# MLP and SwiGLU stages with two classical tile pairs instead of four, and seven-product units behind them

## The chip, the cores and the metric

The kernel runs on one core of a Trainium2 chip. Its time is device microseconds of one execution, from the first to the last instruction with what lies around them; of several runs the median is taken. TensorE (PE in the rows) multiplies, VectorE (DVE) and ScalarE (ACT) work on tiles of 128 partitions, GpSimd (POOL) issues accumulating DMAs and SyncE (SP) plain ones. Each engine works through its own list of instructions in order and waits on semaphores for the others.

## What is computed

Two networks, one after the other, on a sequence of 512 tokens with 1024 channels, in float32. The change touches four places of it, two squared-relu MLPs and two SwiGLU layers:

```python
def squared_relu_mlp(h, w_up, w_down):
    u = jax.nn.relu(h @ w_up)              # 1024 -> 4096, in both layers of the first block
    return (u * u) @ w_down
...
def swiglu_ffn(x, g, w_gate, w_up, w_down):
    h = rms_norm_2(x, g)
    return (jax.nn.silu(h @ w_gate) * (h @ w_up)) @ w_down   # 1024 -> 2816, before and after the mixer
```

Each is added to the residual stream, and before the second network there is a norm with its own gain. Around them stand a stick-breaking attention, a retention layer and a mixer, which the change leaves as they are.

## The kernel before

Activations lie transposed: a tile is 128 channels by 512 tokens, and the stream is eight tiles `hh[0]` to `hh[7]`. Every float32 operand is split into a rounded high part (ScalarE, `whi` or `.hi`) and the remainder (VectorE, `wlo` or `.lo`), and a product is three matmuls, high by low, low by high and high by high (`mm3`, lines 125 to 127).

A **classical tile** (`g_unit`) is 8 k-tiles by 3 matmuls with 512 columns; a pair of tiles is 48 of these. A **unit** (`w_unit`) makes a pair of tiles by the seven products of a Strassen-Winograd scheme on 2 by 2 blocks: seven products, each 4 k-tiles by 3 matmuls with 256 columns, 84 in all, accumulated in four PSUM banks (`ps_z`) with copies between banks on ScalarE (`before(x)`, L337 to L345). It needs two kinds of operands made of sums. The weight side is summed for each panel: two sums by accumulating DMAs from GpSimd (L210, L211), two by VectorE (L263), each then split (L272, L232). The activation side is made once for a stage by `w_operands`, in four groups of two k-tiles: ScalarE lifts two tiles by their gain (L496), VectorE makes four sums (L310 to L313), ScalarE rounds two (L316, L317), VectorE makes two remainders (L319, L320). `w_operands` is a generator with four steps for each group. The weave calls it at every `WT`-th step of the main program; a step is one k-tile of a classical tile (three matmuls) or half a product of a unit (six matmuls).

In a stage the first tile pairs are classical, since the operands for units are not there yet: all four pairs of an MLP's first group of eight tiles, and the first four gate-and-up pairs (`GC`) of a SwiGLU. After them what is left of `w_operands` is drained (`for _ in ops: pass`), and all later pairs are units. The finish of a tile (`up_done`: in an MLP relu L549, square L550, split L172 and L173; in a SwiGLU L1004 to L1006 and the split) is put off by `later` for a few steps. The norm's factor comes while the first tiles run: a sum over partitions on TensorE (L444), a reciprocal root in some twenty tiny VectorE instructions (L425 to L431), a spread over the partitions on TensorE (L437), a copy on ScalarE (L473).

In the first SwiGLU stage, `residual` multiplies the eight tiles of the stream by a second norm's factor (L1789) when the operands are drained (`after()`).

Where an instruction stands in its engine's list is decided by a scheduling framework from dependencies and the order of the program; the lists below come from the built programs. Weight panels are loaded two ahead into three buffers (`RAWS = 3`), and their preparation runs up to `WAHEAD = 5` products ahead.

Of the kernel before, what the change touches and what calls it, by code (L numbers as in the profile page):

```python
# [12 lines left out]
ALU = mybir.AluOpType  # L13
# [41 lines left out]

WAHEAD = 5

WT = 3

GC = 4  # L60


CHUNKS = {
# [23 lines left out]
class Builder:  # L87
# [451 lines left out]
    def mlp(self, layer, hh, X, box, nxt):  # L539

        nc = self.nc
        st = {}
        self.norm_soon(st, box)
        U = {}


        def up_done(m, ps):
            z = self.h()
            nc.scalar.activation(z, ps, AF.Relu)  # L549
            nc.scalar.activation(z, z, AF.Square)  # L550
            U[m] = self.split(z)

        def pair_done(m):
            lo, hi = slice(0, 256), slice(256, 512)
            y, z = self.h(), self.h()

            def d11(c11):
                nc.scalar.activation(y[:, lo], c11, AF.Relu)

            def d12(p, q):  # L560
                nc.vector.tensor_tensor(y[:, hi], p, q, ALU.add)
                nc.vector.scalar_tensor_tensor(y, y, 0.0, y, ALU.max, ALU.mult)

            def d22(p, q):
                nc.vector.tensor_tensor(z[:, hi], p, q, ALU.add)

            def d21(c21):
                nc.scalar.activation(z[:, lo], c21, AF.Relu, scale=-1.0)
                nc.scalar.activation(z[:, hi], z[:, hi], AF.Relu, scale=-1.0)
                nc.scalar.activation(z, z, AF.Square)  # L570
                U[m] = self.split(y)
                U[m + 1] = self.split(z)
            return d11, d12, d22, d21

        def down_done(grp, m, ps):
            if "R2" not in st:
                st["R2"] = self.h()
                nc.vector.tensor_tensor(st["R2"], st["R"], st["R"], ALU.mult)
            t = self.h()
            nc.vector.tensor_tensor(t, ps, st["R2"], ALU.mult)  # L580
            nc.vector.tensor_tensor(hh[m], hh[m], t, ALU.add)
            if grp == 3:
                nxt(m)

        T = []
        ops = self.w_operands(X, T, lambda k: self.lifted(hh[k], self.g(f"mlp{layer}", k)))
        banks = self.w_banks(X[0].hi)

        def main():
            for grp in range(4):  # L590
                for m in range(0, 8, 2):
                    if grp == 0:
                        for x in range(2):
                            yield from self.g_unit(f"up{layer}", X[::2] + X[1::2])
                            self.later(up_done, m + x, self.last)
                    else:
                        yield from self.w_unit(f"up{layer}", T, banks, pair_done(m))
                if grp == 0:
                    for _ in ops:
                        pass  # L600
                self.flush()
                W = [U[m] for m in range(8)]
                for m in range(8):
                    yield from self.g_unit(f"dn{layer}", W)
                    self.later(down_done, grp, m, self.last)

        self.weave(main(), [[ops, WT]])
        self.flush()

# [385 lines left out]
    def ffn(self, which, hh, X, st, nxt, lift, after=lambda: None):  # L995
# [49 lines left out]
        def main():  # L1045
            for gi, grp in enumerate((range(0, 8), range(8, 16), range(16, 22))):
                for i in grp:
                    if i < GC:
                        yield from self.g_unit(f"gu{which}", X[::2] + X[1::2])
                        pg = self.last  # L1050
                        yield from self.g_unit(f"gu{which}", X[::2] + X[1::2])
                        self.later(up_done, i, pg, self.last)
                        if i == GC - 1:
                            for _ in ops:
# [20 lines left out]

        self.weave(main(), [[ops, WT]])
        self.flush()
# [589 lines left out]
    def build(self):  # L1667
        nc = self.nc
        P = self.panels
# [6 lines left out]

        def mlp(l):
            for g in range(4):
                P(f"up{l}", range(g * 4, g * 4 + 4), g > 0)
                P(f"dn{l}", range(g * 4, g * 4 + 4))  # L1680

        def ffn(w):
            for g in range(2):
                for i in range(g * 8, g * 8 + 8):
                    P(f"gu{w}", [i], i >= GC)
                P(f"fd{w}", range(g * 4, g * 4 + 4))
            P(f"gu{w}", range(16, 22), True)
            P(f"fe{w}", range(4))

        mlp(0)  # L1690
        for h in range(4):
            P("retqk", [2 * h, 2 * h + 1])
            P("retv", [2 * h, 2 * h + 1])
            P("retg", [2 * h, 2 * h + 1])
            if h >= 2:
                P("reto", range((h - 2) * 4, (h - 2) * 4 + 4))
        mlp(1)
        ffn(1)
        P("small", [0])
# [42 lines left out]
        def ready(gain, X, hh=None):  # L1742

            def f(m, h):
                self.sumsq(box, m, h)
                X.append(self.gain_in(h, self.g(gain, m)))
            return f if hh is None else lambda m: f(m, hh[m])
# [3 lines left out]
        hh = self.sb(ready("mlp0", X))  # L1751
# [33 lines left out]

        def residual():
            R1 = self.bcast(st["r1"])
            for kt in range(KT):
                nc.vector.scalar_tensor_tensor(hh[kt], hh[kt], self.g("fin", kt), R1, ALU.mult, ALU.mult)  # L1789
        self.later(two_norms, lag=N1)  # L1790
        self.later(spread_r, lag=N2)
        X, Y = [], X
# [164 lines left out]
```

## Time and profile before

| | us |
|---|---|
| median of 3 runs (2482.29 to 2485.35) | 2482.47 |
| the profiled execution | 2483.38 |
| its span, first to last instruction | 2481.7 |
| TensorE, VectorE, ScalarE, GpSimd busy | 2458.5, 1723.5, 1253.1, 138.1 |
| mean granted clock of TensorE, of full speed | 0.997 |
| start of the four stages (first ones-matmul, L298) | 294.4, 1040.7, 1381.8, 2129.6 |

The stages begin with two matmuls that fill PSUM banks with ones-products (L298), by which they are found in the timeline. Matmuls are pipelined: the duration in a row is from start to modelled end and overlaps the next, so the pace is read from start to start. The same holds, to a smaller degree, for VectorE and ScalarE.

### The profile page before, as it was taken

Reading aid. Unit: us, or ns where it says so; the run is one execution under the profiler, and the core shown is the slowest. Engines: PE = TensorE matmul, PEld = TensorE weight load, DVE = VectorE, ACT = ScalarE, POOL = GpSimd, SP = SyncE. Lnnn points to the kernel's source line nnn. Section 1 sums busy time; section 2 is a strip of 40 time slices with the busy share of each in tenths; the row PEclk is TensorE's granted clock in tenths of the full one; section 3 lists DMA queues with packets and bytes.
Section 4 is the critical chain, followed back from the end, with each engine's and each line's share of the span. In section 5 each row is a group of like instructions: output and inputs, shape, how many; then the busy total and the mean of one; then the engine's idle time right before and its main releaser. Section 6 shows DMA issues by size and latency. Waiting matters only on the chain.

```text
span 2481.7 us, 35229 instructions
## 1 busy us (share of the span) xinstructions
PE 2458.5 (99%) x13679; PEld 2141.8 (86%) x13679; DVE 1723.5 (69%) x3061; ACT 1253.1 (50%) x2160; POOL 138.1 (6%) x242
## 2 busy tenths in 40 slices
PE   9999999999999999999999999999999999999999
PEld 7888789989888888889989899998877888899998
DVE  7878857657655545657657776768799777666765
ACT  6777655436333323445436544545555454544543
POOL 0000000000000000000000001010000000001010
PEclk9999999999999999999999999999999999999999
DMA  4112144444222222244443445553221122445551
GB/s 172 69 52 85 51 136 129 127 140 131 95 89 86 76 85 98 76 132 131 129 132 127 119 139 158 148 151 115 73 85 68 51 69 85 123 141 157 150 149 73
DMA packets 78511, 273.20 MB, mean 110 GB/s; under 512 B 8836, under 2 KB 9220, under 8 KB 60680
## 3 DMA queue, kind: packets, MB, share of 16 engines
q1 hardware_dynamic: 60912, 239.43, 27.4%
q0 software_dynamic: 17280, 31.46, 7.7%
q8 instruction: 107, 1.75, 0.3%
q14 instruction: 60, 0.49, 0.1%
q10 hardware_dynamic: 152, 0.06, 0.0%
HBM read 268.82 MB, written 2.10 MB: 109 GB/s over the span
## 4 chain that ended last, share of the span: by engine, by line
PE 93%; DVE 3%; ACT 2%; issue 1%; DMA 0%; SPq 0%; DVEq 0%; ACTq 0%
PE ps_m L125 20%; PE ps_m L126 20%; PE ps_m L127 20%; PE ps_z L125 9%; PE ps_z L127 9%; PE ps_z L126 9%; PE ps_z L134 1%; PE ps_z L796 1%; PE ps_o L437 1%; DVE wlo L241 1%; PE ps_z L135 1%; PE ps_z L797 1%; PE ps_o L444 1%; ACT whi L240 0%; DVE h L1399 0%
## 5 line engine op out<-in xcount | busy, mean ns | idle before, releaser
L125 PE MATMUL ps_m<-h,whi 128*128 128x512 f32 (+1 forms) x2114 | 831.2, 393 | 7.1 <-DVE h L1191 3.5
L126 PE MATMUL ps_m<-h,wlo 128*128 128x512 f32 (+1 forms) x2114 | 826.0, 391 | 0.0
L127 PE MATMUL ps_m<-h,whi 128*128 128x512 f32 (+1 forms) x2114 | 825.0, 390 | 0.0
L240 ACT ACTIVATE whi<-raw 128x1024 fp32r<-128x1024 f32 (+2 forms) x297 | 309.7, 1043 | 580.8 <-PE ps_m L127 493.4
L125 PEld LDWEIGHTS ps_m<-h,whi 128*128 128x128 f32 x2114 | 398.1, 188 | 89.3 <-issue 6.6
L241 DVE TENSOR_TENSOR wlo<-raw,whi 128x1024 fp32r<-128x1024 f32 (+2 forms) x297 | 357.0, 1202 | 166.2 <-ACT whi L240 131.8
L127 PEld LDWEIGHTS ps_m<-h,whi 128*128 128x128 f32 x2114 | 398.1, 188 | 83.3
L126 PEld LDWEIGHTS ps_m<-h,wlo 128*128 128x128 f32 x2114 | 398.5, 189 | 76.9 <-issue 1.2
L125 PE MATMUL ps_z<-h,whi 128*128 128x256 f32 x840 | 237.8, 283 | 1.2 <-ACT h L345 1.2
L125 PE MATMUL ps_z<-h,wlo 128*128 128x256 f32 x840 | 237.7, 283 | 0.0
L126 PE MATMUL ps_z<-h,wlo 128*128 128x256 f32 x840 | 237.7, 283 | 0.0
L127 PE MATMUL ps_z<-h,whi 128*128 128x256 f32 x840 | 237.7, 283 | 0.0
L127 PE MATMUL ps_z<-h,wlo 128*128 128x256 f32 x840 | 237.7, 283 | 0.0
L126 PE MATMUL ps_z<-h,whi 128*128 128x256 f32 x840 | 237.7, 283 | 0.0
L125 PEld LDWEIGHTS ps_z<-h,whi 128*128 128x128 f32 x840 | 161.2, 192 | 1.8 <-ACT h L345 1.4
L126 PEld LDWEIGHTS ps_z<-h,whi 128*128 128x128 f32 x840 | 161.2, 192 | 0.4
L125 PEld LDWEIGHTS ps_z<-h,wlo 128*128 128x128 f32 x840 | 161.3, 192 | 0.0
L126 PEld LDWEIGHTS ps_z<-h,wlo 128*128 128x128 f32 x840 | 161.3, 192 | 0.0
L127 PEld LDWEIGHTS ps_z<-h,wlo 128*128 128x128 f32 x840 | 161.3, 192 | 0.0
L127 PEld LDWEIGHTS ps_z<-h,whi 128*128 128x128 f32 x840 | 161.2, 192 | 0.0
L580 DVE TENSOR_TENSOR h<-ps_m,h 128x512 f32<-128x512 f32 x64 | 44.3, 692 | 152.7 <-PE ps_m L127 152.7
L272 ACT ACTIVATE wlo<-raw 128x512 fp32r<-128x512 f32 x120 | 75.0, 625 | 148.8 <-PE ps_m L126 127.9
(338 smaller groups left out, 3664.8 us busy)
## 6 DMA issues: line engine op xcount, KB each, us to landing
raw<-dn SPq DMA_DIRECT2D x32, 1024.0 KB, 4.8
raw<-gu SPq DMA_DIRECT2D x72, 256.0 KB, 4.4
raw<-gu SPq DMA_DIRECT2D x36, 512.0 KB, 4.4
raw<-fd SPq DMA_DIRECT2D x16, 1024.0 KB, 4.8
raw<-up SPq DMA_DIRECT2D x48, 256.0 KB, 4.5
raw<-up SPq DMA_DIRECT2D x24, 512.0 KB, 4.5
raw<-gu POOLq DMA_DIRECT2D x36, 256.0 KB, 4.1
h<-gu SPq DMA_DIRECT2D x36, 256.0 KB, 4.7
```

The source lines that it names most:

```text
L125: mm(ps, lhs.hi, rhs.lo, start=first, stop=False, skip_group_check=skip)
L126: mm(ps, lhs.lo, rhs.hi, start=False, stop=False, skip_group_check=skip)
L127: mm(ps, lhs.hi, rhs.hi, start=False, stop=last, skip_group_check=skip)
L134: mm(ps, stack, rhs.lo, start=first, stop=False)
L135: mm(ps, stack, rhs.hi, start=False, stop=last)
L240: nc.scalar.activation(hi[:, a:b], r[:, a:b], AF.Copy)
L241: nc.vector.tensor_tensor(lo[:, a:b], r[:, a:b], hi[:, a:b].bitcast(F32), ALU.subtract)
L272: self.nc.scalar.activation(t[:, 0:512], src, AF.Copy)
L437: self.nc.tensor.matmul(ps[:p, tt * 128:(tt + 1) * 128], cols(tt), self.ident, start=tt == 0, stop=tt == 3)
L444: self.nc.tensor.matmul(ps[:, c:c + n], src[:, tt * 128:(tt + 1) * 128], rhs, start=first and tt == 0, stop=last and tt == 3, skip_group_c ...
L580: nc.vector.tensor_tensor(t, ps, st["R2"], ALU.mult)
L796: mm(dst, lhs, src.lo[:, s0:s1], start=False, stop=False, skip_group_check=True)
```

## The change

`GC` goes from 4 to 2 and holds for the MLP as well: two pairs are classical, in all four stages, and the pairs after them are units. The operands are drained after the second pair. `WT` goes from 3 to 2, so `w_operands` takes a step at every second step of the main program. The panel list follows. The eight residual products of the first SwiGLU stage are no longer issued at once, but put off by 6, 12, ... 48 steps.

```diff
--- before.py
+++ after.py
@@ -55,9 +55,9 @@
 
 WAHEAD = 5
 
-WT = 3
-
-GC = 4
+WT = 2
+
+GC = 2
 
 
 CHUNKS = {
@@ -589,15 +589,15 @@
         def main():
             for grp in range(4):
                 for m in range(0, 8, 2):
-                    if grp == 0:
+                    if grp == 0 and m < 2 * GC:
                         for x in range(2):
                             yield from self.g_unit(f"up{layer}", X[::2] + X[1::2])
                             self.later(up_done, m + x, self.last)
+                        if m == 2 * GC - 2:
+                            for _ in ops:
+                                pass
                     else:
                         yield from self.w_unit(f"up{layer}", T, banks, pair_done(m))
-                if grp == 0:
-                    for _ in ops:
-                        pass
                 self.flush()
                 W = [U[m] for m in range(8)]
                 for m in range(8):
@@ -1676,7 +1676,8 @@
 
         def mlp(l):
             for g in range(4):
-                P(f"up{l}", range(g * 4, g * 4 + 4), g > 0)
+                for i in range(g * 4, g * 4 + 4):
+                    P(f"up{l}", [i], i >= GC)
                 P(f"dn{l}", range(g * 4, g * 4 + 4))
 
         def ffn(w):
@@ -1785,8 +1786,11 @@
 
         def residual():
             R1 = self.bcast(st["r1"])
+
+            def one(kt):
+                nc.vector.scalar_tensor_tensor(hh[kt], hh[kt], self.g("fin", kt), R1, ALU.mult, ALU.mult)
             for kt in range(KT):
-                nc.vector.scalar_tensor_tensor(hh[kt], hh[kt], self.g("fin", kt), R1, ALU.mult, ALU.mult)
+                self.later(one, kt, lag=6 * kt + 6)
         self.later(two_norms, lag=N1)
         self.later(spread_r, lag=N2)
         X, Y = [], X
```

TensorE's list grows from 13,527 to 13,815 instructions, VectorE's from 3,015 to 3,099, ScalarE's from 2,116 to 2,188, GpSimd's by 16 and SyncE's by 24.

The built lists show what moves. The first place is ScalarE's list in the first group of the second MLP stage, before: the finish of two tiles (L549, L550, L172), the last group's two lifts (L496), weights rounded for classical tiles (L240), and its rounding (L316, L317).

```order
L549 ACTIVATE h_9539<-ps_m_9474 128x512
L240 ACTIVATE whi_9596<-raw_9321 128x1024
L550 ACTIVATE h_9539<-h_9539 128x512
L172 ACTIVATE h_9542<-h_9539 128x512
L496 ACTIVATE h_9563<-h_2303,gains_92 128x512
L496 ACTIVATE h_9565<-h_2305,gains_92 128x512
L240 ACTIVATE whi_9642<-raw_9448 128x1024
L549 ACTIVATE h_9589<-ps_m_9520 128x512
L550 ACTIVATE h_9589<-h_9589 128x512
L172 ACTIVATE h_9592<-h_9589 128x512
L316 ACTIVATE h_9603<-h_9577 128x512
L317 ACTIVATE h_9605<-h_9578 128x512
```

After, from the same last group's lifts on (the relu there reads the third tile, `ps_m_9585`); `ps_z_9436` and `ps_z_9437` are banks of the first unit:

```order
L496 ACTIVATE h_9650<-h_2303,gains_92 128x512
L496 ACTIVATE h_9652<-h_2305,gains_92 128x512
L549 ACTIVATE h_9660<-ps_m_9585 128x512
L550 ACTIVATE h_9660<-h_9660 128x512
L172 ACTIVATE h_9663<-h_9660 128x512
L316 ACTIVATE h_9682<-h_9670 128x512
L317 ACTIVATE h_9684<-h_9671 128x512
L272 ACTIVATE wlo_9696<-h_9694 128x512
L272 ACTIVATE wlo_9726<-raw_9457 128x512
L549 ACTIVATE h_9735<-ps_m_9643 128x512
L550 ACTIVATE h_9735<-h_9735 128x512
L341 ACTIVATE ps_z_9437<-ps_z_9436 128x256
```

Before, the two lifts stand ahead of one classical weight row and one finish, and a product bank is nowhere near; after, the roundings of weights for units (L272) and a bank's copy (L341) follow directly, and the finish of the fourth tile (`h_9735`) stands ahead of the copy.

The second place is VectorE's list at the same point, from the third group's last remainder to the fourth's, before:

```order
L320 TENSOR_TENSOR h_9527<-h_9509,h_9526 128x512
L310 TENSOR_TENSOR h_9577<-h_9563 128x256
L311 SCALAR_TENSOR_TENSOR h_9578<-h_9577,h_9565 128x256
L313 TENSOR_TENSOR h_9578<-h_9565,h_9563 128x256
L312 SCALAR_TENSOR_TENSOR h_9577<-h_9578,h_9565 128x256
L241 TENSOR_TENSOR wlo_9643<-raw_9448,whi_9642 128x1024
L173 TENSOR_TENSOR h_9593<-h_9589,h_9592 128x512
L319 TENSOR_TENSOR h_9604<-h_9577,h_9603 128x512
L320 TENSOR_TENSOR h_9606<-h_9578,h_9605 128x512
```

and after:

```order
L320 TENSOR_TENSOR h_9629<-h_9615,h_9628 128x512
L232 TENSOR_TENSOR whi_9751<-raw_9457,whi_9751 128x512
L173 TENSOR_TENSOR h_9664<-h_9660,h_9663 128x512
L310 TENSOR_TENSOR h_9670<-h_9650 128x256
L313 TENSOR_TENSOR h_9671<-h_9652,h_9650 128x256
L311 SCALAR_TENSOR_TENSOR h_9671<-h_9670,h_9652 128x256
L312 SCALAR_TENSOR_TENSOR h_9670<-h_9671,h_9652 128x256
L263 TENSOR_TENSOR h_9694<-h_9609,raw_9364 128x512
L319 TENSOR_TENSOR h_9683<-h_9670,h_9682 128x512
L320 TENSOR_TENSOR h_9685<-h_9671,h_9684 128x512
```

Before, the finish of a tile (L173) stands behind the four sums (L310 to L313); after the change it stands ahead of them, so that the sums come after that tile's relu, square and rounding. The weight sum L263 and a weight remainder L232 stand there now in place of the remainder for a classical weight (L241).

The third place is TensorE's list where the last operand group (`h_9604`, `h_9603` before; `h_9683` to `h_9685` after) is read first, in the second MLP stage's first unit. Before, some 400 matmuls after the stage's start:

```order
L125 MATMUL ps_z_9299<-h_9525,wlo_9920 128x256
L126 MATMUL ps_z_9299<-h_9524,wlo_9920 128x256
L127 MATMUL ps_z_9299<-h_9524,wlo_9920 128x256
L125 MATMUL ps_z_9299<-h_9604,wlo_9920 128x256
L126 MATMUL ps_z_9299<-h_9603,wlo_9920 128x256
L127 MATMUL ps_z_9299<-h_9603,wlo_9920 128x256
L125 MATMUL ps_z_9300<-h_9374,whi_9941 128x256
```

and after, 138 matmuls behind the ones-matmuls (beside the norm's sum and spread):

```order
L127 MATMUL ps_z_9434<-h_9284,wlo_9638 128x256
L125 MATMUL ps_z_9434<-h_9361,wlo_9638 128x256
L125 MATMUL ps_z_9436<-h_9629,whi_9611 128x256
L126 MATMUL ps_z_9436<-h_9628,whi_9611 128x256
L127 MATMUL ps_z_9436<-h_9628,whi_9611 128x256
L126 MATMUL ps_z_9434<-h_9360,wlo_9638 128x256
L127 MATMUL ps_z_9434<-h_9360,wlo_9638 128x256
L125 MATMUL ps_z_9434<-h_9431,wlo_9638 128x256
L126 MATMUL ps_z_9434<-h_9430,wlo_9638 128x256
L127 MATMUL ps_z_9434<-h_9430,wlo_9638 128x256
L125 MATMUL ps_z_9435<-h_9683,wlo_9580 128x256
L126 MATMUL ps_z_9435<-h_9682,wlo_9580 128x256
```

Before, the unit's rows stand in the order of the products. After, rows of a later product (`wlo_9638` into `ps_z_9434`) are placed between those that wait for the third and fourth group, and the rows on the fourth group come last ahead of the product that needs the bank's copy (`ps_z_9437`).

## Rows read from the trace of the kernel before

**Rows 1.** Page: span; busy time, share and instructions of each engine.

```profile
span 2481.7 us, 35229 instructions
PE 2458.5 (99%) x13679; PEld 2141.8 (86%) x13679; DVE 1723.5 (69%) x3061; ACT 1253.1 (50%) x2160; POOL 138.1 (6%) x242
```

**Rows 2.** Page: chain that ended last, by engine.

```profile
PE 93%; DVE 3%; ACT 2%; issue 1%; DMA 0%; SPq 0%; DVEq 0%; ACTq 0%
```

**Rows 3.** Windows: length, busy time by engine, granted clock, DMA share, GB/s.

```profile
1041.00:1130.00 89.00, 89.00 (x402) 73.74 (x401) 49.81 (x84) 41.68 (x62) 5.17 (x6) 1.00 0.37 110
...
1430.00:1471.00 41.00, 39.79 (x333) 39.59 (x332) 37.10 (x66) 25.56 (x50) 1.72 (x2) 1.00 0.45 142
```

**Rows 4.** Timeline (start, duration, instruction), TensorE: first and last of 133 classical matmuls.

```profile
310.50 0.40 PE L125 MATMUL ps_m<-h,whi 128*128 128x512 f32 x1
...
340.43 0.39 PE L125 MATMUL ps_m<-h,whi 128*128 128x512 f32 x1
```

**Rows 5.** Timeline, first SwiGLU stage: residual block, 33 unit matmuls, a wait.

```profile
1431.02 5.38 DVE L1789 SCALAR_TENSOR_TENSOR h<-h,gains 128x512 f32<-128x512 f32 x8
...
1434.74 0.28 PE L125 MATMUL ps_z<-h,wlo 128*128 128x256 f32 x1
...
1438.58 0.28 PE L127 MATMUL ps_z<-h,wlo 128*128 128x256 f32 x1
1440.07 0.38 PE L125 MATMUL ps_z<-h,whi 128*128 128x256 f32 x1 [1.21 <-ACT h L345]
```

**Rows 6.** Timeline, TensorE, first SwiGLU stage: the norm's spread.

```profile
1394.82 0.39 PE L127 MATMUL ps_m<-h,whi 128*128 128x512 f32 x1
1395.54 0.68 PE L437 MATMUL ps_o<-ident,c 128*128 128x128 f32 x4 [0.33 <-DVE c L1781]
```

**Rows 7.** Timeline, second MLP stage: its start, the spread and its copy.

```profile
1040.69 0.64 PE L298 MATMUL ps_z<-h,onesr 128*128 128x512 f32 x2
...
1048.98 1.13 PE L437 MATMUL ps_o<-ident,c 128*128 128x128 f32 x8
1050.14 0.60 ACT L473 ACTIVATE h<-ps_o 128x512 f32<-128x512 f32 x1 [1.23 <-PE ps_o L437]
```

**Rows 8.** Timeline, ScalarE, second MLP stage.

```profile
1064.63 0.63 ACT L316 ACTIVATE h<-h 128x512 fp32r<-128x512 f32 x1 [2.22 <-DVE h L312]
1065.16 0.62 ACT L317 ACTIVATE h<-h 128x512 fp32r<-128x512 f32 x1
...
1068.31 1.32 ACT L496 ACTIVATE h<-h,gains 128x512 f32<-128x512 f32 x2
...
1071.52 0.58 ACT L549 ACTIVATE h<-ps_m 128x512 f32<-128x512 f32 x1
...
1073.33 0.61 ACT L316 ACTIVATE h<-h 128x512 fp32r<-128x512 f32 x1
```

**Rows 9.** Timeline, VectorE, second MLP stage.

```profile
1062.44 0.69 DVE L173 TENSOR_TENSOR h<-h 128x512 fp32r<-128x512 f32 x1
...
1064.17 0.42 DVE L312 SCALAR_TENSOR_TENSOR h<-h 128x256 f32<-128x256 f32 x1
...
1073.46 0.69 DVE L173 TENSOR_TENSOR h<-h 128x512 fp32r<-128x512 f32 x1 [0.46 <-ACT h L172]
1074.07 0.68 DVE L319 TENSOR_TENSOR h<-h 128x512 fp32r<-128x512 f32 x1
```

**Rows 10.** Windows in the mixer: a hole of TensorE, and what follows it.

```profile
1846.00:1849.00 3.00, 0.03 (x1) 0.06 (x1) 2.87 (x7) 1.67 (x3) 0.00 (x0) 0.59 0.00 0
1849.00:1852.00 3.00, 3.00 (x7) 2.42 (x8) 2.90 (x7) 2.50 (x4) 0.00 (x0) 0.50 0.00 0
```

**Rows 11.** Groups by line (busy, mean ns, idle before), and an issue's landing.

```profile
L263 DVE TENSOR_TENSOR h<-raw 128x512 f32<-128x512 f32 x60 | 41.0, 684 | 0.0
...
L210 POOL DMA_DIRECT2D raw<-up x24 | 20.9, 869 | 597.0 <-DMA raw<-up 476.6 <-DVE h L580 53.9 <-issue 40.2
...
raw<-up SPq DMA_DIRECT2D x48, 256.0 KB, 4.5
```

## The prediction

> **What bounds the kernel now.** I read the page's busy line first: the profiled execution has a span of 2481.7 us, and TensorE is busy in 99% of it, VectorE in 69%, ScalarE in 50% [rows 1]. The chain of waits says the same from the other side: 93% of what ended last is matmul, 3% VectorE, 2% ScalarE [rows 2]. So time is won only by fewer or cheaper matmuls, and lost wherever TensorE stands still. Then I looked at the four stages that the change touches, by windows: in the second MLP stage's first group TensorE has no idle time at all, while VectorE is busy 49.8 and ScalarE 41.7 of 89 us [rows 3]. There the unit operands are made with a lot of room. In the first SwiGLU stage TensorE has lost a little [rows 3]; the timeline shows the two places, a spread of the norm that came late [rows 6] and a unit that waited for a copy while VectorE ran eight residual products in one block [rows 5].
>
> **What is removed: matmul time.** A classical pair of tiles is 48 matmuls with 512 columns; 132 of them in a row take 340.43 − 310.50 = 29.93 us, 0.2267 each [rows 4], so a pair takes 10.88 us. A unit is 84 matmuls with 256 columns, at (1438.58 − 1434.74) / 32 = 0.120 us [rows 5], 10.08 us. Two pairs in each of four stages become units (TensorE's listing grows by 288 = 8 × 36 matmuls, as it should), so 8 × 0.80 = 6.4 us go, if nothing waits. The Trainium skill (TensorE: Matmul & The Clock Gate, "Wait — 56ns, not 53.3ns?") gives a full-clock matmul its columns over 2.4 GHz plus about 2.5 ns, which would be 0.2158 and 0.1092 us; an estimate from it is 8 × (10.36 − 9.17) = 9.5 us saved, and the forecast would be 3.1 us lower. The rows above contradict it here, by 5% at 512 columns and by 10% at 256, and the sum goes by the rows.
>
> **What goes in the first SwiGLU stage.** The wait for the spread was 1395.54 − 1394.82 less one matmul, 0.49 us [rows 6]. The block of eight residual products, 5.38 us of VectorE, came just before a wait of 1440.07 − 1438.58 − 0.12 = 1.37 us [rows 5]. After the change the eight stand six steps of the weave or more apart. The cover is VectorE's room among units: 37.1 us in the 41 us window of four units holds the block itself [rows 3], so a unit needs (37.1 − 5.4) / 4 = 7.9 of its 10.08 us, and one residual product of 0.67 in every 6 steps × 0.72 = 4.3 us fits. Without that cover they cost up to 5.4 us. I count both old waits as gone, 1.9 us, and put what replaces them below.
>
> **What is added beside TensorE.** A unit's panel needs three more loads on SyncE's queue and two accumulating ones on GpSimd, 0.86 us of GpSimd each [rows 11]. Panels are fetched two ahead, some 21.8 us of matmuls, against two landings of about 4.5 us one after the other [rows 11] and two issues; I count nothing, and if that cover is gone, up to 4 us at a stage's first unit. The third term is VectorE's and ScalarE's own: it decides the case.
>
> **What is late now: the operands.** A stage makes four operand groups, one for two X tiles. Before, the last is finished at 1074.07 + 0.68 in the second MLP stage [rows 9], 34 us after its start [rows 7], and the first unit reads it 55 us later. Now TensorE reaches the row that reads the last group after 2 ones-matmuls, 96 matmuls of 512 columns, the norm's sum and spread, and 42 matmuls of 256: 0.48 + 21.8 + 0.8 + 0.9 + 5.0 = 29.0 us after the start (sum and spread are eight short matmuls each; the spread's merged row is 1.13 less the tail that the next matmul overlaps [rows 7], and the sum's are a little shorter). Everything that doesn't need the last group is already placed ahead of it, so nothing is left to fill a wait.
>
> When is it ready? The orders on ScalarE and VectorE are fixed, and each operand group stands behind the finish of a tile. I walk one pass by rows of before. Two lifts on ScalarE take 1.23 (a merged row of 1.32, less its tail) [rows 8]; then the tile's finish, relu, square and split, goes over to VectorE's L173 at 1073.46 − 1071.52 = 1.94 [rows 8, 9]; from L173 over the four sums to ScalarE's L316 it is 1064.63 − 1062.44 = 2.19 [rows 8, 9]; L316 to L317 0.53, and 0.53 again to the next lift [rows 8]. That is 5.9 to L317 and 6.4 for a pass, while TensorE needs 5.44 for a tile. Before, a pass was asked for only every 12 steps of 0.68, in 8.2 us; now it is every 8.
>
> The walk starts where ScalarE copies the norm's spread, because the second group's lifts stand behind that copy. In the second MLP stage the spread moved behind 43 matmuls: 0.48 + 43 × 0.2267 + 0.8 = 11.0, and the copy starts 1.16 later [rows 7], at 12.2. Then 0.5 for the copy; 6.4 + 0.5 for the first pass (a weight row of 0.54 is between); 6.4 + 0.7 + 0.6 + 0.5 for the second (a weight sum L263 of 0.68 [rows 11], a weight remainder and a weight rounding); for the third 1.23 + 1.94 + 2.19 and 0.74 from L316 to L319 [rows 8, 9], 6.1; and 0.75 until L319 has ended. Sum 22.5, so the last group is there at 34.7, and TensorE stands for 34.7 − 29.0 = **5.7 us**. In the first MLP stage the spread stands behind 62 matmuls, at 15.3, the copy at 16.5; the passes are 6.4, 8.0 and 6.1, with copy and end 21.7, ready at 38.2: **9.2 us**. After each, the second operand of the group, 12 more matmuls' result and one copy on ScalarE, behind two rows of another tile, cost 1.2 more before the next product may start: 2.4.
>
> In the SwiGLU stages only one of the three passes has a tile's finish in it, so the walk is shorter. By the same distances a pass without it is about 3.5 us, since the sums start behind the first lift, and the one with it 9.3: five dependent rows at 0.65, and the weight sum, remainder and rounding. In the second SwiGLU stage the spread is behind 42 matmuls and the copy at 12.0; with 0.5 + 3.5 + 9.3 + 3.6 + 0.7 the group is ready at 29.6 against 29.0, 0.6 us, and a copy wait of 0.7 follows: **1.3**. In the first it is 56 matmuls and two sums, the copy at 15.9, and a middle pass of 8.1: ready at 32.3 against 30.7 (two sums, two spreads), 1.6; the spread itself is late by 0.5 as before, and two copy waits are 0.5 and 0.6: **3.2**.
>
> Bounds, since no row shows these waits: each is nothing if the two queues overlap fully, and the walk is the upper end for MLP (9.2 and 5.7); for SwiGLU I take 0 to 5. Below nothing they can't go, as TensorE's own rows are counted in full. I take the walk's values, since every link in it has a row from the same stage.
>
> **The clock after a hole.** Between 1846 and 1849 TensorE was busy 0.03 us, and in the 3 us that followed its granted clock was 0.50, the 1.2 GHz level, and seven matmuls took 0.43 instead of 0.23 [rows 10]: 1.4 us. The hole of 1.37 us had no such effect (the matmuls behind it kept 0.120). Holes of five us and more in both MLP stages should do the same: 2 × 1.4 = 2.8, with 0 and 5 as the ends.
>
> **Sum.** −6.4 − 1.9 + 9.2 + 5.7 + 2.4 + 1.3 + 3.2 + 2.8 = +16.3 us. The profiled execution took 2483.4 us (span 2481.7 and 1.7 around it), so 2499.7; the median of the three runs shown is 0.9 lower, which makes **2498.8**. A change of less than 0.2%, 5.0 us, can't be told from none by this measurement.
>
> **Rivals.**
> *The queues keep up.* VectorE and ScalarE have half their time free [rows 3]; counted without any waiting, the 50 to 70 rows of VectorE up to the last operand, at 0.6 us for 512 columns and 0.35 for 256 [rows 9], come to some 21 to 27 us of the 29. Then only the cut shows: 2482.5 − 6.4 − 1.9 = 2474.2. Against it: the two queues wait for each other four times a pass, which a busy share doesn't show. 9%.
> *Half the wait.* The finish of a tile is ready long before its turn, and if ScalarE runs it while VectorE is still at the last group, a pass is 6.4 − 1.9 = 4.5; three passes are 5.8 shorter, MLP waits 3.4 + 0 + 1.2, holes too short to touch the clock: −8.3 + 4.6 + 4.5 = +0.8, 2483. For it: the relu's input is there early. Against it: the orders place the lifts before the finish, and L173 before the sums. 15%.
> *The hole is not the end.* While the operands are made, the weights of the first two units are made late as well, so every product of these units waits for its remainder row; VectorE's room of 2.2 us a unit gives back a backlog of 5 us only over two units. Decides if VectorE enters the first unit with less than one product prepared: 4 stages × 2.5 more, 2509. 12%.
> That units don't replace pairs is excluded by the listing (288 matmuls, above).
>
> **Chances and range.** My forecast 64%, the others as above. Slower by over 0.2% is the forecast and the last rival, 0.76; within 0.2% is half the wait, 0.15; faster 0.09. The forecast's own range is 2489 to 2507, by the ends of the MLP waits and the clock; with half the wait taken in, eight times in ten the time lies between 2483 and 2507.
>
> **What would show it.** In the timeline of the changed kernel: holes of TensorE just ahead of the rows that read the last operand group, each ended by VectorE's L319 or L320, some 9 us in all in the first and 6 in the second MLP stage, under 4 in SwiGLU; 0.50 in the clock row behind the long ones; passes of 6 to 8 us between the L320 rows. No long wait before a residual product's neighbour. If the four first units run without a gap of over 1 us, the walk is wrong and the time is near 2474; if gaps lie in later products, the third rival has it.

## The result, and the profile after

The changed kernel takes 2503.7 us (median of four runs, 2502.47 to 2503.85), the kernel before 2482.78 beside it: a ratio of 1.0082, interval 1.007 to 1.0094. It is slower by 20.9 us. 2498.8 was forecast, in a range of 2483 to 2507.

The page of the changed kernel: span, busy line, chain by engine.

```profile
span 2502.1 us, 36050 instructions
...
PE 2464.0 (98%) x13967; PEld 2157.2 (86%) x13967; DVE 1755.7 (70%) x3145; ACT 1275.8 (51%) x2232; POOL 152.2 (6%) x258
...
PE 91%; DVE 5%; ACT 3%; issue 1%; DMA 0%; SPq 0%; ACTq 0%; DVEq 0%
```

Against [rows 1, 2] the busy shares hardly moved. What tells is the chain: TensorE's share of it is two points lower, VectorE's two and ScalarE's one higher. TensorE's busy time even grew by 5.5 us, though its matmuls should have become 6.4 cheaper: part of them ran at half the clock. Busy shares would not have found this.

The landmarks on TensorE (the ones-matmuls at a stage's start, the sum of the mixer's norm) cut the two profiled executions into stretches:

| stretch | before | after | difference | forecast |
|---|---|---|---|---|
| start to the first MLP | 294.41 | 292.75 | -1.66 | 0 |
| first MLP, and on to the second | 746.28 | 757.03 | +10.75 | +10.2 |
| second MLP | 341.09 | 348.57 | +7.48 | +6.7 |
| first SwiGLU | 355.06 | 355.89 | +0.83 | -0.3 |
| mixer | 392.76 | 395.45 | +2.69 | 0 |
| second SwiGLU and end | 352.07 | 352.37 | +0.30 | -0.3 |

TensorE's timeline in the first MLP stage (start, duration, instruction, in brackets the idle time before it and what ended it); the stage starts at 292.75:

```profile
320.84 0.28 PE L127 MATMUL ps_z<-h,wlo 128*128 128x256 f32 x1
321.95 0.38 PE L125 MATMUL ps_z<-h,whi 128*128 128x256 f32 x1 [0.83 <-ACT whi L272]
322.90 0.39 PE L126 MATMUL ps_z<-h,whi 128*128 128x256 f32 x1 [0.56 <-DVE whi L232]
...
325.04 0.39 PE L125 MATMUL ps_z<-h,wlo 128*128 128x256 f32 x1 [1.28 <-DVE h L319]
...
331.16 0.58 PE L125 MATMUL ps_z<-h,wlo 128*128 128x256 f32 x1 [4.90 <-DVE h L319]
...
333.42 0.58 PE L125 MATMUL ps_z<-h,whi 128*128 128x256 f32 x1 [0.60 <-ACT ps_z L341]
...
337.07 0.28 PE L127 MATMUL ps_z<-h,wlo 128*128 128x256 f32 x1
```

The same in the second MLP stage, which starts at 1049.78:

```profile
1079.30 0.28 PE L127 MATMUL ps_z<-h,wlo 128*128 128x256 f32 x1
1084.29 0.48 PE L125 MATMUL ps_z<-h,wlo 128*128 128x256 f32 x1 [4.71 <-DVE h L319]
...
1086.54 0.58 PE L125 MATMUL ps_z<-h,whi 128*128 128x256 f32 x1 [0.64 <-ACT ps_z L341]
...
1091.46 0.28 PE L127 MATMUL ps_z<-h,wlo 128*128 128x256 f32 x1
```

The reader sees a hole ended by L319, the remainder of the last operand group, and behind it a smaller one ended by a bank's copy. In the first stage the weights of the first unit are late as well (L272, L232), 1.4 us in all, and so is the third operand group (1.28). From the first row shown to the last it is 16.23 us for 36 matmuls in the first stage and 12.16 us for 30 in the second. At 0.120 each they would take 4.3 and 3.6, so 11.9 and 8.6 us are lost there; less the 1.6 us that two units save, that is 10.3 and 7.0 of the 10.75 and 7.48 in the table.

ScalarE in the second MLP stage of the changed kernel, to lay beside [rows 7, 8]:

```profile
1062.20 0.60 ACT L473 ACTIVATE h<-ps_o 128x512 f32<-128x512 f32 x1 [2.66 <-PE ps_o L437]
1062.70 1.33 ACT L496 ACTIVATE h<-h,gains 128x512 f32<-128x512 f32 x2
...
1069.50 1.32 ACT L496 ACTIVATE h<-h,gains 128x512 f32<-128x512 f32 x2
...
1077.52 1.33 ACT L496 ACTIVATE h<-h,gains 128x512 f32<-128x512 f32 x2
1078.75 0.59 ACT L549 ACTIVATE h<-ps_m 128x512 f32<-128x512 f32 x1
...
1082.88 0.63 ACT L316 ACTIVATE h<-h 128x512 fp32r<-128x512 f32 x1 [2.22 <-DVE h L312]
```

And VectorE there, answering to [rows 9]:

```profile
1080.69 0.69 DVE L173 TENSOR_TENSOR h<-h 128x512 fp32r<-128x512 f32 x1 [1.78 <-ACT h L172]
1081.30 0.42 DVE L310 TENSOR_TENSOR h<-h 128x256 f32<-128x256 f32 x1
...
1083.55 0.69 DVE L319 TENSOR_TENSOR h<-h 128x512 fp32r<-128x512 f32 x1
1084.15 0.69 DVE L320 TENSOR_TENSOR h<-h 128x512 fp32r<-128x512 f32 x1
```

From lift to lift the passes are 6.8 and 8.0 us. In the last one both engines stand idle in turn, ScalarE 2.22 before L316 and VectorE 1.78 before L173, while TensorE waits for both. L319, for which TensorE's row waits, ends 34.46 us after the stage's start, L320 35.06.

The windows of the changed kernel (length, busy time by engine, granted clock, DMA share, GB/s) over the two holes and what follows each, to lay beside [rows 10]:

```profile
1079.00:1084.20 5.20, 0.58 (x5) 0.38 (x4) 3.38 (x8) 2.91 (x6) 0.00 (x0) 1.00 0.00 0
1084.20:1091.20 7.00, 6.27 (x28) 5.98 (x29) 5.45 (x10) 5.40 (x12) 0.00 (x0) 0.52 0.41 150
326.10:331.10 5.00, 0.16 (x2) 0.00 (x0) 3.50 (x9) 2.71 (x6) 0.00 (x0) 0.56 0.00 0
331.10:336.90 5.80, 5.13 (x22) 4.84 (x23) 4.51 (x9) 4.99 (x12) 0.00 (x0) 0.50 0.53 186
```

By these rows the clock is at its 1.2 GHz level for 5.8 us behind the first hole (and for most of that hole: 0.56) and for 6.7 us behind the second, and a matmul of 256 columns takes 0.213 from start to start in place of 0.120.

The first SwiGLU stage has the late spread, as in [rows 6], and two copy waits:

```profile
1413.97 1.13 PE L437 MATMUL ps_o<-ident,c 128*128 128x128 f32 x8 [0.37 <-DVE c L1782]
...
1429.26 0.39 PE L125 MATMUL ps_z<-h,whi 128*128 128x256 f32 x1 [1.19 <-ACT ps_z L337]
...
1433.67 0.39 PE L125 MATMUL ps_z<-h,whi 128*128 128x256 f32 x1 [0.46 <-ACT ps_z L341]
```

The second has two copy waits of 0.46. In the first the wait beside the residual block [rows 5] is gone.

The two stretches outside the four stages have the same instructions in the same order on TensorE. What differs there is where and for how long the clock was at its lower level. In the stretch ahead of the first MLP, before and after:

```profile
279.00:287.00 8.00, 7.35 (x23) 5.80 (x22) 3.40 (x6) 2.42 (x5) 0.00 (x0) 0.57 0.00 0
279.00:287.00 8.00, 8.00 (x31) 6.46 (x30) 5.08 (x9) 3.85 (x7) 1.76 (x2) 0.79 0.50 81
```

In the mixer, before:

```profile
1925.00:1930.00 5.00, 4.84 (x31) 4.11 (x30) 4.55 (x9) 4.92 (x10) 0.68 (x3) 0.84 0.00 0
1930.00:1935.00 5.00, 5.00 (x23) 4.14 (x22) 2.88 (x10) 0.40 (x1) 0.31 (x2) 0.81 0.00 0
```

after, 17.4 us later in the program:

```profile
1942.40:1947.40 5.00, 4.90 (x28) 4.61 (x29) 4.51 (x8) 4.35 (x9) 0.59 (x2) 0.72 0.00 2
1947.40:1952.40 5.00, 5.00 (x17) 4.23 (x17) 1.14 (x4) 0.53 (x1) 0.41 (x2) 0.50 0.00 0
1952.40:1957.40 5.00, 5.00 (x22) 4.11 (x21) 4.03 (x15) 0.00 (x0) 0.00 (x0) 0.76 0.00 0
```

By their clock, these rows hold some 3.5 us at the lower level before and 10 after; the rows ahead of the first MLP hold 6.9 before and 3.4 after. Over the thirteen profiled executions of this case the mixer took 392.8 to 393.8 us in eight and 395.3 to 395.6 in five, whatever was changed outside it. Differences of 2.5 us there say nothing of a kernel.

### The profile page after: what moved, and what is told of

The parts are those of the page before. It is cut to its first block, busy times and chain, and to the rows that moved or that the text cites. A ratio compares the mean times of both kernels' runs of the same rounds, so it can differ in the third digit from the quotient of the medians.

```text
span 2502.1 us, 36050 instructions
## 1 busy us (share of the span) xinstructions
PE 2464.0 (98%) x13967; PEld 2157.2 (86%) x13967; DVE 1755.7 (70%) x3145; ACT 1275.8 (51%) x2232; POOL 152.2 (6%) x258
## 4 chain that ended last, share of the span: by engine, by line
PE 91%; DVE 5%; ACT 3%; issue 1%; DMA 0%; SPq 0%; ACTq 0%; DVEq 0%
PE ps_m L125 18%; PE ps_m L126 18%; PE ps_m L127 18%; PE ps_z L125 10%; PE ps_z L127 10%; PE ps_z L126 10%; PE ps_z L796 1%; PE ps_z L134 1%; PE ps_z L797 1%; PE ps_o L444 1%; DVE wlo L241 1%; PE ps_z L135 1%; PE ps_o L437 1%; ACT h L496 0%; DMA raw<-sbv 0%
## 5 line engine op out<-in xcount | busy, mean ns | idle before, releaser
L125 PE MATMUL ps_m<-h,whi 128*128 128x512 f32 (+1 forms) x1986 | 781.4, 394 | 6.4 <-DVE h L1191 3.6
L126 PE MATMUL ps_m<-h,wlo 128*128 128x512 f32 (+1 forms) x1986 | 776.0, 391 | 0.0
L127 PE MATMUL ps_m<-h,whi 128*128 128x512 f32 (+1 forms) x1986 | 775.4, 391 | 0.0
L240 ACT ACTIVATE whi<-raw 128x1024 fp32r<-128x1024 f32 (+2 forms) x281 | 292.9, 1043 | 561.3 <-PE ps_m L127 475.9
L125 PEld LDWEIGHTS ps_m<-h,whi 128*128 128x128 f32 x1986 | 374.2, 188 | 84.1 <-issue 6.6
L127 PEld LDWEIGHTS ps_m<-h,whi 128*128 128x128 f32 x1986 | 373.9, 188 | 78.2
L241 DVE TENSOR_TENSOR wlo<-raw,whi 128x1024 fp32r<-128x1024 f32 (+2 forms) x281 | 337.5, 1201 | 142.8 <-ACT whi L240 105.5
L126 PEld LDWEIGHTS ps_m<-h,wlo 128*128 128x128 f32 x1986 | 374.4, 189 | 71.6 <-issue 1.2
L125 PE MATMUL ps_z<-h,wlo 128*128 128x256 f32 x952 | 271.4, 285 | 11.0 <-DVE h L319 10.9
L125 PE MATMUL ps_z<-h,whi 128*128 128x256 f32 x952 | 272.3, 286 | 4.7 <-ACT ps_z L341 2.2
L126 PE MATMUL ps_z<-h,whi 128*128 128x256 f32 x952 | 270.8, 284 | 0.6 <-DVE whi L232 0.6
L127 PE MATMUL ps_z<-h,whi 128*128 128x256 f32 x952 | 270.7, 284 | 0.0
L126 PE MATMUL ps_z<-h,wlo 128*128 128x256 f32 x952 | 270.2, 284 | 0.0
L127 PE MATMUL ps_z<-h,wlo 128*128 128x256 f32 x952 | 270.0, 284 | 0.0
L125 PEld LDWEIGHTS ps_z<-h,wlo 128*128 128x128 f32 x952 | 183.6, 193 | 12.5 <-DVE h L319 12.1
L125 PEld LDWEIGHTS ps_z<-h,whi 128*128 128x128 f32 x952 | 183.8, 193 | 8.1 <-ACT ps_z L341 3.1
L126 PEld LDWEIGHTS ps_z<-h,whi 128*128 128x128 f32 x952 | 184.0, 193 | 1.3 <-DVE whi L232 0.8
L127 PEld LDWEIGHTS ps_z<-h,whi 128*128 128x128 f32 x952 | 184.0, 193 | 0.0
L126 PEld LDWEIGHTS ps_z<-h,wlo 128*128 128x128 f32 x952 | 183.6, 193 | 0.0
L127 PEld LDWEIGHTS ps_z<-h,wlo 128*128 128x128 f32 x952 | 183.5, 193 | 0.0
L272 ACT ACTIVATE wlo<-raw 128x512 fp32r<-128x512 f32 x136 | 85.0, 625 | 156.6 <-PE ps_m L126 132.5
```

The lines of the kernel that those rows point to most:

```text
L125: mm(ps, lhs.hi, rhs.lo, start=first, stop=False, skip_group_check=skip)
L126: mm(ps, lhs.lo, rhs.hi, start=False, stop=False, skip_group_check=skip)
L127: mm(ps, lhs.hi, rhs.hi, start=False, stop=last, skip_group_check=skip)
L240: nc.scalar.activation(hi[:, a:b], r[:, a:b], AF.Copy)
L241: nc.vector.tensor_tensor(lo[:, a:b], r[:, a:b], hi[:, a:b].bitcast(F32), ALU.subtract)
L272: self.nc.scalar.activation(t[:, 0:512], src, AF.Copy)
```

## Experiments

Theory: in the MLPs the last operand group is late, because its passes start at the copy of the norm's spread and have tile finishes in front; the hole then costs a second time by the clock. Rivals: the weights of the first units are late; the loss lies in all four stages; the copy is idle time anyway. Stages are compared by the stretches of the table above, each run by its profiled execution. Where a run's edit adds lines near the top of the kernel, its line numbers are higher than those in the text: by one with `GM` alone (L126 for L125, L273 for L272, L550 for L549, L1005 for L1004), by four with the fillers (L323 for L319).

| run | median us | ratio to before, interval |
|---|---|---|
| two pairs in the MLPs alone | 2504.05 | 1.0087, 1.0073 to 1.0101 |
| two pairs in the SwiGLUs alone | 2489.19 | 1.0027, 1.0016 to 1.0037 |
| norm put off | 2496.54 | 1.0054, 1.0042 to 1.0067 |
| `WT` = 1 | 2487.64 | 1.0019, 1.001 to 1.0028 |
| three pairs | 2487.06 | 1.0016, 1.0008 to 1.0025 |
| mixed | 2479.64 | 0.9986, 0.9977 to 0.9995 |
| `WT` = 3 | 2491.8 | 1.0035, 1.0022 to 1.0047 |
| `WT` = 1, lifts on GpSimd | 2504.67 | 1.0086, 1.0073 to 1.01 |
| filler | 2498.39 | 1.0066, 1.0053 to 1.008 |
| residual alone | 2481.18 | 0.9994, 0.9985 to 1.0002 |
| mixed, second version | 2478.43 | 0.9982, 0.9973 to 0.999 |

**MLPs alone** (the changed kernel with a constant `GM` = 2 for the MLPs, `GC` = 4, the residual block as before):

```diff
-GC = 2
+GC = 4
+GM = 2
...
-                self.later(one, kt, lag=6 * kt + 6)
+                one(kt)
```

> Two classical pairs in the MLPs alone; the SwiGLUs keep four, and the residual products stand in one block again (WT = 2 stays). From the changed kernel's trace the first MLP stage and what follows it to the second is 10.75 us longer than before, the second 7.5. Walk theory (the wait for the last operand group in the two MLPs is nearly the whole loss): 2482.8 + 18.2 = 2501, within 2. Rival (the loss is spread over all four stages, or comes with WT = 2 and the residual products): 2490 to 2495.

Measured: 2504.05, all of the loss, and 3 more than expected. The MLPs show the same long holes (5.1 and 5.0 us from start to start). The SwiGLUs did not return to their old time (+1.9 and +0.5 against before): with four pairs at `WT` = 2 and the residual block, TensorE waits for a rounded weight in both (1.47 and 1.01 us, L273). The profiled execution took 2508.64, 4.6 over the median. Behind its two holes the clock stayed at the lower level for some 8.5 us each, longer than in the changed kernel, and its two MLP stretches are 1.15 and 0.62 us longer:

```profile
332.90:341.40 8.50, 7.88 (x35) 7.59 (x36) 6.09 (x11) 6.03 (x14) 0.00 (x0) 0.50 0.38 127
1087.20:1096.00 8.80, 8.12 (x37) 7.83 (x38) 6.39 (x13) 6.33 (x15) 0.00 (x0) 0.52 0.33 119
```

**SwiGLUs alone** (`GC` = 2, `GM` = 4, residual products spread).

> Two classical pairs in the SwiGLUs alone, four in the MLPs; residual products spread, WT = 2. Walk theory: the 3.2 us of matmuls and the two old waits of 1.9 are gone, the new waits are 2.8 in the first and 1.6 in the second SwiGLU, and the trace of the changed kernel has these stages 0.8 and 0.3 longer: 2483 to 2484, not to be told from before. Rival (weights late, or the residual products costing VectorE 5 us): 2487 or more. Rival (queues keep up): 2478.

Measured: 2489.19, above the walk's 2484 and in the range of the first rival, but by neither of the causes that it named. The stretches show why: first SwiGLU with mixer +1.2, second +0.1, second MLP 0.0, and the *first MLP* +5.5, though it makes four classical pairs as before. Its waits on TensorE (engine, line, what was waited for, us, times, longest):

```profile
PE ps_m L126 <- ACT h L550: 4.1, 4, 1.5
```

`WT` = 2 alone costs this: on ScalarE each pass's lifts now stand ahead of a tile's relu (L549, L550 in this run), the relu frees a PSUM tile, and there are three of these. So `WT` trades one wait for another, and these two parts don't add up to the change (+21.1 and +6.3 against +20.9).

**The norm put off**, in the two MLPs:

```diff
-        self.norm_soon(st, box)
+        self.norm_soon(st, box, 40, 46)
```

> The changed kernel, with the norm's sum put off to step 40 and its spread to step 46 in the two MLPs (nothing reads the factor before the first down projection). In ScalarE's list only the copy of the spread leaves its place ahead of the second group's lifts. Walk theory (the passes start at that copy): the second lifts come 5.0 and 3.2 us earlier, and some 3 more since the tiny VectorE instructions no longer stand ahead of the first sums; 1.7 us of short matmuls leave the time before the wait. Holes of about 3 and 1 us instead of 9 and 6, half-clock stretches gone or shorter: 2488 to 2493. Rival (the finishes alone set the pace, the copy is idle time anyway): 2501 to 2504. Rival (weights late): the holes now end with a weight row, 2500.

Measured: 2496.54, 7.2 us faster than the changed kernel; the first MLP 4.3, the second 3.15 us shorter. The second group's lifts start 4.8 and 4.2 us earlier, as the theory has it, so "idle time anyway" falls. It gave less than expected, since the put-off norm came back in a worse place. TensorE in the second MLP stage:

```profile
1076.23 1.13 PE L437 MATMUL ps_o<-ident,c 128*128 128x128 f32 x8 [1.56 <-DVE c L431]
1077.91 0.39 PE L125 MATMUL ps_z<-h,wlo 128*128 128x256 f32 x1 [0.55 <-DVE h L319]
...
1080.17 0.39 PE L125 MATMUL ps_z<-h,whi 128*128 128x256 f32 x1 [1.03 <-ACT ps_z L341]
```

and in the first, where the spread itself is the long wait:

```profile
325.62 1.49 PE L437 MATMUL ps_o<-ident,c 128*128 128x128 f32 x8 [3.69 <-DVE c L431]
```

The tiny VectorE instructions of the norm now run among the last group's sums, and the spread stands on TensorE just ahead of the row that waits.

**`WT` = 1:**

```diff
-WT = 2
+WT = 1
```

> The changed kernel with WT = 1: the operands take a step at every step of the main program. In ScalarE's list one tile's finish stands ahead of the last group instead of three; the other finishes then stand ahead of the first bank's copy. Walk theory (finishes ahead of the groups make the passes 6 to 8 us): last group ready at 28 and 25 us after the start, so its hole is gone; the copy is late instead, by 5 and 2 us: 2486 to 2495. If the copy waits for nothing: 2480. Rival (weights late): 2500 or more, holes ended by weight rows.

Measured: 2487.64. The last group is ready 29.4 and 23.1 us after the start (28 and 25 expected), and it ends no wait of over 0.2 us in either MLP. The second MLP is 7.25 us shorter than in the changed kernel, with one copy wait of 1.45 left. The first is only 3.0 shorter:

```profile
325.55 0.58 PE L125 MATMUL ps_z<-h,whi 128*128 128x256 f32 x1 [2.97 <-ACT whi L272]
...
330.49 0.58 PE L125 MATMUL ps_z<-h,whi 128*128 128x256 f32 x1 [1.50 <-ACT ps_z L341]
```

There the weights and then the copy are late: the rival's mechanism, but only once the operands are out of the way. So the theory holds, with the rival right behind it in the first MLP.

**Three pairs** in all four stages (`GC` = 3).

> Three classical pairs in all four stages, WT = 2, residual products spread. Walk theory: the last operand group is needed 10.9 us later (about 40 us after the start) and is ready at 31 to 39, so no hole before it and no half-clock stretch behind; -3.2 us of matmuls, -1.4 of old waits, and in the first MLP stage 2 to 4 us of waits for a PSUM tile whose finish stands behind operand rows (4.1 us with four pairs at WT = 2): 2480 to 2483. Rival (weights of the first units are late): holes of some 5 us in both MLPs, ended by weight rows: 2488 or more.

Measured: 2487.06, 4 to 7 us over what was expected. The second MLP (-0.4) and the second SwiGLU (-1.6) came out as the theory has it; the first MLP lost 5.4, about what `WT` = 2 alone cost it with four pairs (5.5):

```profile
313.89 0.50 PE L126 MATMUL ps_m<-h,whi 128*128 128x512 f32 x1 [0.85 <-ACT h L550]
...
336.90 0.38 PE L126 MATMUL ps_z<-h,whi 128*128 128x256 f32 x1 [1.70 <-ACT whi L273]
```

The PSUM wait is smaller than I put it, and the first unit's weights are late by 1.7 and 0.34, with the clock at its lower level for 3.4 us behind them. The first MLP has not shown room for units in its first group, with two pairs or three. In the first SwiGLU two waits are left, for the spread (0.52) and for a finish (1.25, L1005).

**Mixed**: each stage by what the runs so far point to.

```diff
-WT = 2
+WT = 1
+WM = (3, 1)
...
+GM = (4, 3)
```

(`GM` and `WM` hold for the first and second MLP; the SwiGLUs keep `GC` = 2 and take `WT` = 1.)

> The parts put together by stage: first MLP as before (four pairs, WT = 3), second MLP three pairs at WT = 1, both SwiGLUs two pairs at WT = 1, residual products spread. Walk theory, by the stages of the WT = 1 run (first SwiGLU to the mixer and on -0.7, second -1.9 against before) and -0.8 for one pair in the second MLP: 2482.8 - 3.4 = 2479.4. Rival (what a stage loses depends on the stage before it, or on the clock's phase): 2482 or more.

Measured: 2479.64, on the expected time, and faster than before by 0.14%, clear of noise. So here the stages could be chosen one by one.

**`WT` = 3** in the changed kernel.

> The changed kernel with WT = 3. ScalarE's list has two tiles' finishes in the passes of the second and third group, and none in the fourth, where the changed kernel has one in each. Walk theory: the last pass is 2 us shorter in both MLPs, the rest the same: 2498 to 2501. Rival (the operands are asked for too late, so WT decides): later by a step in every group, 2508 or more.

Measured: 2491.8, 6 us under the expected range. The MLP part was right: the last group is ready 2.6 and 1.65 us earlier and the two stages are 2.6 and 2.5 shorter. I had overlooked the SwiGLUs, which gained 2.2 and 1.0 more (the longest wait left in the first is a copy's, 0.46); 2.5 is the mixer's clock. In both MLPs a hole of 2.8 us ended by L319 is left. A later call of the operands put them at a better place than `WT` = 2, and `WT` = 1 is better than both. So by these three values it isn't only how early they are asked for, but what stands in front of each.

**Lifts on GpSimd**, with `WT` = 1:

```diff
-        self.nc.scalar.activation(y, x, AF.Copy, scale=g)
+        self.nc.gpsimd.tensor_scalar(y, x, g, None, ALU.mult)
```

> WT = 1 with the eight lifts of a stage made by GpSimd instead of ScalarE. Theory that at WT = 1 ScalarE's whole list up to the first bank copy is the bound (47 rows in 40 us in the first MLP): eight rows of 0.62 go, 5 us, so the 5.5 us of holes in the first MLP and the 1.5 in the second fall to 1 or nothing: 2480 to 2483. Rival (the chain of one operand group is the bound, and a lift on GpSimd, of which no row of before tells the price, is slower and stands in it): 2488 to 2500.

Measured: 2504.67, 17 us worse than with ScalarE. Groups by line of this run (busy, mean ns of one, idle before):

```profile
L496 POOL TENSOR_SCALAR h<-h,gains 128x512 f32<-128x512 f32 x24 | 43.8, 1937 | 6.5 <-DVE h L656 6.5
...
L319 DVE TENSOR_TENSOR h<-h 128x512 fp32r<-128x512 f32 x16 | 13.9, 867 | 7.3 <-ACT h L316 7.3
```

A lift takes 1.94 us there against 0.71 on ScalarE, and VectorE's L319 rises from 689 to 867 ns. The norm's spread was late by 4.55 and 5.99 us in the SwiGLUs. Whether ScalarE's whole list is the bound in the first MLP isn't shown, but the run speaks against it: with eight rows fewer on that list TensorE has the same two waits there, 2.97 for L272 and 1.50 for L341.

**Filler**, in the changed kernel's MLPs:

```diff
-    def w_operands(self, X, T, lift):
+    def w_operands(self, X, T, lift, fill=0):
...
+            if i == 3 and fill:
+                ps = self.ps("o")
+                for _ in range(fill):
+                    self.nc.tensor.matmul(ps, self.ones, y1, start=True, stop=True)
...
```

(the MLPs call it with `fill=5`)

> The changed kernel with five more matmuls of 512 columns, whose result nothing reads, on the last group's lifted tile in each MLP stage: they run in the holes of 5.2 and 5 us. Theory that the hole costs twice, by its length and by the half-clock stretch behind it (the rows at 0.213 in place of 0.120 add up to 1.7 us in the first MLP and 2.1 in the second): the holes are filled, the clock stays at 1.00, and 3 to 5 us come back: 2499 to 2501. Rival (the slow rows behind the hole have another cause, or the fillers run past it): 2504 or more.

Measured: 2498.39, 5.3 faster with more work. The stretches: first MLP -1.7, second -2.2, mixer -1.8 (phase), SwiGLUs 0.0. The five make ten instructions in a stage. Their row in the first MLP:

```profile
325.37 6.14 PE L311 MATMUL ps_o<-h,ones 128*128 128x512 f32 x10
```

Windows of this run over both stages:

```profile
322.00:326.00 4.00, 2.32 (x10) 1.63 (x11) 3.69 (x7) 3.97 (x8) 0.00 (x0) 0.92 0.00 0
326.00:330.00 4.00, 4.00 (x7) 1.58 (x6) 2.80 (x7) 1.74 (x4) 0.00 (x0) 0.65 0.01 4
1080.00:1084.00 4.00, 2.95 (x16) 1.88 (x14) 3.78 (x7) 3.22 (x7) 0.00 (x0) 1.00 0.38 113
1084.00:1088.00 4.00, 3.59 (x30) 3.60 (x31) 3.07 (x6) 3.83 (x11) 0.00 (x0) 1.00 0.36 150
```

In the second MLP the clock stays at 1.00. In the first it fell, by these windows, at about 325.4, as the fillers began: what lay ahead of the fall were the three short waits, not the long hole. It was back at 328.8, before the row that had waited. So 3.9 us of the two MLPs' loss go with the clock behind the holes, since the operands came no earlier (the last L320 ends 38.9 and 35.05 us after the stages' starts, against 38.96 and 35.06). This is a lower bound: in the first stage the fillers ran 0.9 us past the point at which the row could have started (39.3 us after the stage's start, 38.4 in the changed kernel).

**Residual products alone**, spread in the kernel before.

> The kernel before, with the eight residual products of the first SwiGLU stage spread over six steps each, and nothing else of the change. Theory of the prediction: the wait of 1.37 us goes and nothing takes its place: 2481.3, too little to tell from before by the median, but the timeline of the stage has no wait over 0.5 us there. Rival (the products crowd the units' rows on VectorE): the wait moves or grows, 2483 or more.

Measured: 2481.18, and the first SwiGLU is 1.49 us shorter. The median can't tell it from before; in the timeline the wait of 1.2 us has gone, and the only one named in the 80 us from the stage's start is the late spread (0.32).

**Mixed, second version:** `WT` = 3 in the first SwiGLU.

```diff
+WF = {1: 3, 2: 1}
```

> The mixed kernel with WT = 3 in the first SwiGLU stage, where the run with WT = 3 had no wait over 0.3 us and the mixed one had 1.16, 0.48 and 0.32. Walk theory: up to 1.5 us less in that stage: 2478 to 2479.5. Rival (those waits are hidden or come back elsewhere): 2479.6.

Measured: 2478.43; the first SwiGLU takes 353.12 us against 354.43 in the first mixed version. (The run with `WT` = 3 did have one wait over 0.3 us there, a copy's 0.46, and it is here too.) This is the best of all, 4.1 us under the kernel before.

## Why the prediction was right

**Matmul time** (-6.4): right where no wait hides it. The second MLP of the mixed kernel has one pair fewer and no wait, and is 0.82 us shorter than before, with 0.80 forecast. The second SwiGLU with `WT` = 1 is 1.9 us shorter, 1.6 of which are its two units.

**The walk** was right in the MLPs. It gave the copy of the spread at 16.5 and 12.2 us after the start, measured 16.9 and 12.4, and the end of the last L319 at 38.2 and 34.7, measured 38.4 and 34.5. The passes of 6.4 and 8.0 us in the first and 6.9 and 8.2 in the second came out at 6.4, 7.8, 6.8 and 8.0. Moving the copy (norm put off) brought the end of the last group forward by 4.3 and 2.5 us, and `WT` = 1, with fewer finishes ahead of it, by 9.6 and 12.0. In the SwiGLUs the walk was short by more: 32.3 and 29.6, measured 33.6 and 30.3. One reading was loose: the row that the prediction takes as the last of before [rows 9] is L319, and L320 ends 0.6 us behind it.

**The waits by stage.** +10.2 and +6.7 were forecast for the MLPs, +10.75 and +7.48 measured; for the SwiGLUs -0.3 and -0.3, measured +0.83 and +0.30. The residual step was right (1.49 against 1.4). Inside the MLPs the agreement is in part luck. From start to start, the waits up to the last group's row cost 8.3 us in the first (in four places, two of them waits for weights) and 4.9 in the second, where 9.2 and 5.7 were forecast; TensorE came to that row at 29.6 in the second stage, not 29.0. A copy's wait cost 0.9, not 1.2. Slow rows and restarts cost 2.7 in each stage, not 1.4. The misses go both ways and nearly cancel.

In the SwiGLUs the forecast had TensorE wait 1.6 and 0.6 us for the operands. No wait of over 0.15 us is ended by them there: TensorE had already been held by a copy (L337, 1.19 and 0.46), which the sum didn't have at that place. Their totals were off by 1.1 and 0.6 us, and the mechanism was another.

**The clock** was the term of the wrong size: 2.8 forecast from the 1.4 us of the mixer's hole [rows 10], at least 3.9 measured by the filler. The stretch behind the MLP holes lasts some 6 to 7 us, not 3: that row covered only its first part.

**The rest** of the 4.9 us by which the time is above the forecast: +1.0 outside the four stages by the clock's phase (-1.66 and +2.69), 1.1 and 0.6 in the SwiGLUs, 0.55 and 0.8 in the MLPs (the clock's 1.1 or more, less what the holes fell short), and 0.8 because the profiled execution of before lay 0.9 above its median and that of the changed kernel only 0.15.

**The rivals.** "The queues keep up" fell with the first hole: engines busy for half the time still came 5 us late, as each waits for the other inside a pass. "Half the wait" needed passes of 4.5 us, with the finishes behind the lifts' sums; the lists fixed that they aren't, and the passes took 6.4 to 8.0. "The weights late" was half right: present in the first MLP at 1.4 us, and the next limit there as soon as the operands come in time.

**What the prediction took as given** was `WT` = 2. Much of the loss hangs on it: with the same two pairs the four stages lose 19.4 us by their stretches at `WT` = 2, 11.1 at `WT` = 3 and 4.5 at `WT` = 1. Calling the operands more often, which was meant to have them earlier, put a tile's finish ahead of the sums of the last group, where `WT` = 3 has none.

## What to carry to other kernels

When work on the bounding engine is brought forward, compute when its last operand is *ready* by walking the in-order lists of the engines that make it, link by link; busy shares of 50% hid a chain that was 5 to 8 us too long. Replace classical work by cheaper work stage by stage, since the room in front of each differs: two units in place of pairs cost 8 to 11 us in the first MLP at the three values of `WT`, and in the second SwiGLU, with the operands called at every step, they gained 2. In this kernel a hole of some 5 us on TensorE cost about 2 us more behind it.

## What the runs showed of the hardware

- More matmuls made the kernel faster: 20 instructions whose result nothing reads gave back 3.9 us in the MLPs; the clock stayed at its 2.4 GHz level in the second and was back at it sooner in the first.
- Three waits of 0.83, 0.56 and 1.28 us within 4 us stood ahead of the drop of the clock in the first MLP; one of 1.37 alone had no drop behind it [rows 5].
- The mixer's half-clock stretch came out at some 3.5 and at some 10 us for the same instructions in the same order. Behind the MLP holes it lasted some 6 to 7 us in one execution and 8.5 in another.
- GpSimd's lift slows VectorE beside it. Of the sixteen L319 rows of that run, the twelve beside no lift took 0.68 or 0.69 us, the four beside one 1.02, 1.14, 1.61 and 1.82. The Trainium skill ("SBUF — State Buffer", "Who interferes with whom") says that a VectorE instruction with two inputs in SBUF contends with a GpSimd instruction that reads SBUF, and that the ports they share are an exclusive lock. The trace agrees in kind: L319 has two such inputs, and its worst row is longer by 1.13 us, less than one whole lift of 1.94.
